# RWKV-7 chunks: a head-pair state without its zero blocks, multiplied in two row halves with one PSUM bank per head

## The chip, the cores and the metric

The kernel runs on one core of one Trainium2 chip. The metric is the device time of one execution in microseconds (us), taken as the median of several runs. TensorE is called PE here, its weight load PEld, VectorE DVE, ScalarE ACT, GpSimd POOL, and SyncE SP.

## What is computed

The reference is a two-layer trunk of width 1024 over 512 tokens. Each layer projects its input with one large matrix, runs two token mixers on the parts (HGRN2 and RWKV-7), gates and merges them, projects again and normalises. The change touches RWKV-7, which has 8 heads of 64 channels, each with a state of 64x64:

```python
def step(S, inp):                       # S_t = S_{t-1}(diag(w) - kk^T (a*kk)) + v^T k ; y = S r
    r_t, w_t, k_t, v_t, kk_t, a_t = inp
    sa = jnp.einsum('bhvk,bhk->bhv', S, -kk_t)
    S = (S * w_t[:, :, None, :] + sa[..., None] * (kk_t * a_t)[:, :, None, :]
         + v_t[..., None] * k_t[:, :, None, :])
    y = jnp.einsum('bhvk,bhk->bhv', S, r_t)
    return S, y
```

The kernel computes this in 8 chunks of 64 tokens per layer: within a chunk everything is matrix products, and the state goes from chunk to chunk.

## The kernel before

**The work and its order.** One Python program writes out all instructions for the two layers. The bulk of TensorE's work is the projections: `proj` (L258) multiplies a weight tile by all 512 tokens in 24 matmuls of 512 columns each (L267, L268, L272), with weights split into a high and a low part by ACT (L122) and POOL (L127, `wl`). These projections serve as filler: `weave` (L283) takes a number of filler matmuls from a list of counts, then lets the main generator issue its next piece. For the chunks the counts are `WCH` (L33): 0, 3, 3, 1, 7, 5, 5 filler matmuls before the pieces of one chunk, 24 in all. Each engine runs its own instructions in the order written, so the filler stands on TensorE's queue between the products of the chunk.

**One chunk** (`rw_chunk`, L571) handles 8 heads as 4 pairs (`p` is the pair, `h` the head in it; head `h` has its 64 channels in row half `64*h`). Its pieces, by line:

- L589: 8 products `pg`, 64 rows each, the two heads of a pair in two PSUM banks; DVE masks them into `Gt` (a tile named G, L592).
- L601: 4 transposes; ACT copies them to `bkt` (L603).
- L608, in chunks 1 to 7: the old state times the queries and keys. The state `mbd` is a tile of 128 rows by 4 pairs by 128 columns; for each pair its two 64x64 blocks stand on the diagonal and the other two blocks are zero (a memset at L1076 in each layer). So one full 128-row matmul of 128 columns serves a pair.
- L613: 8 products of 64x64 added to the same bank `py`; DVE scales one row half of 256 columns at a time into `W` (L618, recorded at the helper L127).
- L623: 8 products with `ar` into `psa`; DVE copies one half into `X`, ACT the other (L625).
- L631, in chunks 0 to 6: 8 products for the state's update, each head's 64x64 result on its diagonal place in the bank `pm`; DVE adds it to `gm` and writes `mbd`, one row half at a time (L638, helper L127; L636 in chunk 0); POOL makes the decayed `gm` from it (L640).
- L643: 8 more products into `py`; ACT copies the result to `X` in two instructions of 64x256 (L647). In every second chunk DVE, POOL and ACT work on from there (L650 to L658), towards the group norm and, after the last chunk, the transposes of `rw_final` (L691).

A 32-bit float product is recorded as two passes, so 8 products are x16 in the trace's rows and the 4 of L608 are x8.

**Tiles and pools.** PSUM has 8 banks in three pools: `pj` 2, `rw` 4, `hg` 2 (L94). `py` is of pool `rw`. The tile `mbd` is also used elsewhere, whole, as a 512-column row of conditioning values (`silc`, L174).

Of the kernel before, what the change touches and what calls it, by code (L numbers as in the profile page):

```python
# [16 lines left out]
ALU = mybir.AluOpType  # L17
# [66 lines left out]
def body(ctx, tc, d):  # L84
    nc = tc.nc
    V, A, G, PE = nc.vector, nc.scalar, nc.gpsimd, nc.tensor
# [10 lines left out]
    def st(tag, shape, dt=F32):  # L97
        cnt[0] += 1
        return sp.tile(shape, dt, tag=tag, name=f"{tag}_{cnt[0]}", bufs=BUFS[tag])

    def ps(tag):
        cnt[0] += 1
        return pp.tile([128, 512], F32, tag=tag, name=f"p{tag}_{cnt[0]}", bufs=PB[tag])
# [13 lines left out]
    def cst(name, shape, dt=F32):  # L117
        return cp.tile(list(shape), dt, name=name)

    def act(out, in_, f, scale=1.0, bias=0.0):  # L120
        if f == AF.Copy:
            A.activation(out, in_, f, scale=scale)  # L122
        else:
            A.activation(out, in_, f, scale=scale, bias=bias)  # L124

    def tt(e, o, a, b, op):
        e.tensor_tensor(o, a, b, op=op)  # L127

    def mul(e, o, a, b):
        tt(e, o, a, b, ALU.mult)  # L130
# [4 lines left out]
    def stt(o, a, s, b, op0, op1):  # L135
        V.scalar_tensor_tensor(o, a, s, b, op0=op0, op1=op1)  # L136

    def bc(ap, n):
        return ap.unsqueeze(len(ap.shape)).broadcast_to(list(ap.shape) + [n])
# [4 lines left out]
    mm = PE.matmul  # L144
# [21 lines left out]
    craw = [ps("rw"), ps("rw")]  # L166
    for h in range(2):
        cmm = mm(craw[h], ones[0:1], crow[:, h * 512:(h + 1) * 512], start=True, stop=True)
    mbd = cst("mbd", (128, 4, 128))
    silc = []  # L170

    def c_rows(craw):

        silc[:] = [mbd.rearrange("p a b -> p (a b)"), st("W", [128, 512])]  # L174
        for h in range(2):
            act(silc[h], craw[h], AF.Tanh, scale=0.5)
            stt(silc[h], silc[h], 1.0, craw[h], ALU.add, ALU.mult)
# [171 lines left out]
    rw = {}  # L349
# [11 lines left out]
    gam = cst("gam", (128, 4, 8))  # L361
    d2 = cst("d2", (128, 4, 4, 2))
# [206 lines left out]
    gm = cst("gm", (128, 4, 64))  # L569

    def rw_chunk(l, c):  # L571


        ytm = rw["ytm"]
        par, c4 = c % 2, c // 2
        yo = [64 * (par ^ g) for g in range(2)]
        yrs, zrs = [slice(y, y + 64) for y in yo], [slice(64 - y, 128 - y) for y in yo]
        halves = [slice(256 * g, 256 * g + 256) for g in range(2)]
        heads = [(p + 2 * g, h) for p in range(2) for h in range(2) for g in range(2)]
        hcol = lambda p, h: slice(p * 128 + h * 64, p * 128 + h * 64 + 64)  # L580
        ch = slice(c * 128, (c + 1) * 128)
        ZR, BK, X = rw["ZR"], rw["BK"], rw["vtm"][c]

        yield
        pg = [ps("rw"), ps("rw")]
        for p in range(4):
            for h in range(2):
                hs = slice(64 * h, 64 * h + 64)
                mm(pg[h][:, p * 128:(p + 1) * 128], BK[p][hs, ch], ZR[p][hs, ch], start=p == 0, stop=p == 3)  # L589
        Gt = st("G", [128, 2, 4, 128])  # L590
        for h in range(2):
            mul(V, Gt[:, h].rearrange("p (g a) b -> p g a b", g=2), pg[h].rearrange("p (g a b) -> p g a b", g=2, b=128),  # L592
                gmask(par))
        bkt = None
        if c < 7:
            sk = st("W", [128, 4, 128])
            mul(G, sk, rw["BKb"].rearrange("p a b c -> p a (b c)")[:, :, ch], bc(gam[:, :, c], 128))
            yield
            pb = ps("rw")
            for p in range(4):  # L600
                PE.transpose(pb[:, p * 128:(p + 1) * 128], sk[:, p], ident)  # L601
            bkt = st("bkt", [128, 512])
            A.copy(bkt, pb)  # L603
        yield
        py = ps("rw")
        if c > 0:
            for p in range(4):
                mm(py[:, p * 128:(p + 1) * 128], ZR[p][:, ch], mbd[:, p], start=p == 0, stop=False)  # L608
        yield
        for n, (p, h) in enumerate(heads):  # L610
            g = p // 2
            z = zrs[g]
            mm(py[z, hcol(p, h)], Gt[yrs[g], h, p, z], X[yrs[g], hcol(p, h)], start=c == 0 and n < 2, stop=n > 5)  # L613
        W = st("W", [128, 512])
        j3 = lambda t: t.rearrange("p (n j) -> p n j", j=64)
        for g in range(2):
            z, o = zrs[g], halves[g]
            mul(V, j3(W[z, o]), j3(py[z, o]), bc(d2[z, c4, 2 * g:2 * g + 2].rearrange("p a b -> p (a b)"), 64))  # L618
        yield
        psa = ps("rw")  # L620
        for n, (p, h) in enumerate(heads):
            z = zrs[p // 2]
            mm(psa[z, hcol(p, h)], ar[z, h, p, c4], W[z, hcol(p, h)], start=n < 2, stop=n > 5)  # L623
        for g in range(2):
            PK[1 - g](X[zrs[g], halves[g]], psa[zrs[g], halves[g]])  # L625
        yield
        if c < 7:
            pm = ps("rw")
            for p in range(4):
                for h in range(2):  # L630
                    mm(pm[64 * h:64 * h + 64, hcol(p, h)], bkt[:, hcol(p, h)], X[:, hcol(p, h)], start=p == 0, stop=p == 3)  # L631
            for h in range(2):
                hs = slice(64 * h, 64 * h + 64)
                new = pm[hs].rearrange("p (a b) -> p a b", b=128)[:, :, hs]
                if c == 0:
                    V.tensor_copy(mbd[hs, :, hs], new)  # L636
                else:
                    tt(V, mbd[hs, :, hs], new, gm[hs], ALU.add)  # L638
                if c < 6:
                    mul(G, gm[hs], mbd[hs, :, hs], bc(gam[hs, :, c + 1], 64))  # L640
        for n, (p, h) in enumerate(heads):
            y = yrs[p // 2]
            mm(py[y, hcol(p, h)], Gt[:, h, p, y], X[:, hcol(p, h)], start=False, stop=n > 5, skip_group_check=True)  # L643
        if par == 0:
            ytm.append(X)
        for g in range(2):
            A.copy(ytm[-1][64 * par:64 * par + 64, halves[g]], py[yrs[g], halves[g]])  # L647
        if par == 1:

            y = ytm[-1]  # L650
            y3 = y.rearrange("p (h j) -> p h j", j=64)
            s1, s2 = st("sm", [128, 8]), rw["s2"][:, c4]
            V.tensor_reduce(s1, y3, axis=AX.X, op=ALU.add)
            V.tensor_scalar_mul(s1, s1, -1.0 / 64)
            tt(G, y3, y3, bc(s1, 64), ALU.add)
            sq = st("bkt", [128, 512])
            act(sq, y, AF.Square)
            V.tensor_reduce(s2, sq.rearrange("p (h j) -> p h j", j=64), axis=AX.X, op=ALU.add)  # L658
# [329 lines left out]
    for l in range(L):  # L988
# [84 lines left out]
                run(fill)  # L1073
            rkv = []
        ada_next()
        G.memset(mbd, 0.0)  # L1076
        inv = rw_invert()
        next(inv)
        weave(hg_norm(l, oT), fill, WHN)
# [291 lines left out]
```

## Time and profile before

| what | value |
|---|---|
| median of 3 runs | 1013.33 us (1008.05 to 1017.07) |
| the profiled execution's own time | 1013.57 us |
| its span from first to last instruction | 1011.8 us |
| mean granted TensorE clock in it | 0.991 of full speed |
| PE busy | 939.3 us (93% of the span) |
| DVE, POOL, ACT busy | 711.7, 632.4, 452.2 us |
| chunks of layer 0, of layer 1 | about 301 to 392 us, about 790 to 881 us |

The rows in the last section but one come from this execution; times in them count from the span's start. A row of a timeline gives start, duration, engine, line, operation, output and inputs; several of a kind are merged with xcount. A matmul's duration is modelled and includes the way through the array, so that successive matmuls overlap in it: what one costs is read from the starts. "idle before" is the time the engine stood still, and the arrow names what ended it.

### The profile page before, as it was taken

To read this page: it belongs to the slowest core of one execution; us is meant where nothing else is said; L and a number is where in the kernel's file an instruction comes from. 1 tells how busy PE (TensorE), PEld (TensorE's weight loads), DVE (VectorE), ACT (ScalarE), POOL (GpSimd) and SP (SyncE) were. 2 spreads that over 40 slices of the span, in tenths; PEclk is the share of its full clock that TensorE was granted. 3 is DMA by queue.
4 is the path that set the end of the run, shared out by engine and by line. 5 is a ranking of instruction groups with operands and counts; after the bars stand their busy time and mean duration, and the time that the engine had idled before them with its cause. 6 is when DMAs were issued, how large, how long until landed. Compare 5 with 4: busy or idle time off the path is not lost.

```text
span 1011.8 us, 17028 instructions
## 1 busy us (share of the span) xinstructions
PE 939.3 (93%) x6132; PEld 751.6 (74%) x6132; DVE 711.7 (70%) x1265; ACT 452.2 (45%) x920; POOL 632.4 (63%) x738
## 2 busy tenths in 40 slices
PE   7877889999999999999989979999999999999997
PEld 3656768887877777776877868778788777787776
DVE  7889997769974443588777895867699344436667
ACT  3356445556334335333445645446632443453421
POOL 5366646556655557768646566666754566686865
PEclk9999999999999999999999999999999999999999
DMA  8824532222321112665632632232233111254322
GB/s 315 306 63 136 177 126 74 88 80 80 97 75 45 52 46 65 186 213 169 186 132 63 205 87 77 70 94 63 64 99 90 53 43 53 85 177 157 115 74 83
DMA packets 61750, 112.85 MB, mean 112 GB/s; under 512 B 6865, under 2 KB 11361, under 8 KB 61666
## 3 DMA queue, kind: packets, MB, share of 16 engines
q1 hardware_dynamic: 57778, 105.12, 34.1%
q10 hardware_dynamic: 3888, 6.64, 2.0%
q8 instruction: 48, 0.79, 0.3%
q14 instruction: 36, 0.29, 0.1%
HBM read 106.49 MB, written 5.25 MB: 110 GB/s over the span
## 4 chain that ended last, share of the span: by engine, by line
PE 47%; DVE 24%; POOL 9%; DMA 7%; issue 7%; ACT 6%; POOLq 0%; SPq 0%; DVEq 0%; ACTq 0%
PE ppj L272 11%; PE ppj L267 10%; PE ppj L268 10%; POOL wl L127 5%; DVE u L127 4%; DVE z L308 2%; DVE B L308 2%; DVE hl L127 2%; DMA raw<-in_w_out 2%; DMA z<-in_w_ada 2%; ACT wh L122 2%; PE prw L589 2%; POOL hl L127 1%; PE prw L608 1%; DVE pu L136 1%
## 5 line engine op out<-in xcount | busy, mean ns | idle before, releaser
L127 POOL TENSOR_TENSOR wl<-raw,wh 128x256 fp32r<-128x256 f32 x460 | 384.5, 859 | 245.1 <-ACT wh L122 158.5
L122 ACT ACTIVATE wh<-raw 128x512 fp32r<-128x512 f32 (+1 forms) x233 | 144.0, 622 | 162.6 <-PE ppj L268 87.2
L267 PE MATMUL ppj<-B,wh 128*128 128x512 f32 x432 | 175.4, 406 | 5.3 <-DVE u L136 2.2
L268 PE MATMUL ppj<-B,wh 128*128 128x512 f32 x432 | 172.3, 399 | 0.0
L267 PE MATMUL ppj<-A,wh 128*128 128x512 f32 x400 | 161.1, 403 | 0.2 <-ACT wh L122 0.2
L268 PE MATMUL ppj<-A,wh 128*128 128x512 f32 x400 | 159.6, 399 | 0.0
L272 PE MATMUL ppj<-B,wl 128*128 128x512 f32 x432 | 125.9, 401 | 0.6 <-DVE dvsh L127 0.4
L272 PE MATMUL ppj<-A,wl 128*128 128x512 f32 x400 | 116.9, 401 | 4.6 <-POOL wl L127 4.6
L267 PEld LDWEIGHTS ppj<-B,wh 128*128 128x128 f32 x432 | 81.9, 190 | 24.0 <-ACT wh L122 3.8
L272 PEld LDWEIGHTS ppj<-B,wl 128*128 128x128 f32 x432 | 80.3, 190 | 19.0 <-POOL wl L127 2.4
L268 PEld LDWEIGHTS ppj<-B,wh 128*128 128x128 f32 x432 | 82.0, 190 | 14.9
L272 PEld LDWEIGHTS ppj<-A,wl 128*128 128x128 f32 x400 | 73.3, 188 | 22.8 <-POOL wl L127 8.1
L267 PEld LDWEIGHTS ppj<-A,wh 128*128 128x128 f32 x400 | 75.5, 189 | 16.0 <-ACT wh L122 0.6
L268 PEld LDWEIGHTS ppj<-A,wh 128*128 128x128 f32 x400 | 75.7, 189 | 13.7
L127 POOL TENSOR_TENSOR hl<-hl,u 128x256 f32<-128x256 f32 x40 | 31.9, 797 | 20.7 <-DVE u L774 7.8
L127 DVE TENSOR_TENSOR W<-prw,d 64x256 f32<-64x256 f32 x32 | 13.5, 422 | 36.9 <-PE prw L613 26.0
L136 DVE SCALAR_TENSOR_TENSOR pr<-ppj,prm,pr 128x511 f32<-128x511 f32 x22 | 16.4, 747 | 31.8 <-ACT pr L124 31.8
L127 DVE TENSOR_TENSOR t<-t,t 128x144 f32<-128x144 f32 (+29 forms) x62 | 35.1, 566 | 2.1
L308 DVE CUSTOM_DVE_ANT_0 z<-z,mbd,prm 128x512 f32<-128x512 f32 x32 | 31.8, 995 | 3.9 <-DMA z<-in_w_ada 3.8
L127 DVE TENSOR_TENSOR hl<-hl,u 128x256 f32<-128x256 f32 x64 | 32.6, 524 | 1.4 <-ACT u L792 1.3
L308 DVE CUSTOM_DVE_ANT_0 z<-z,W 128x512 f32<-128x512 f32 x32 | 29.0, 905 | 2.7 <-DMA z<-in_w_ada 2.7
L127 DVE TENSOR_TENSOR G<-prw,cc 128x512 f32<-128x512 f32 x32 | 20.6, 684 | 12.0 <-PE prw L589 11.8
(480 smaller groups left out, 1967.4 us busy)
## 6 DMA issues: line engine op xcount, KB each, us to landing
raw<-in_w_in SPq DMA_DIRECT2D x182, 256.0 KB, 2.6
z<-in_w_ada SPq DMA_DIRECT2D x64, 256.0 KB, 3.2
B<-in_w_ada SPq DMA_DIRECT2D x16, 512.0 KB, 5.9
raw<-in_w_br SPq DMA_DIRECT2D x32, 256.0 KB, 2.7
raw<-in_w_out SPq DMA_DIRECT2D x32, 256.0 KB, 2.6
u<-in_x SPq DMA_DIRECT2D x8, 256.0 KB, 4.5
o<-in_w_in SPq DMA_DIRECT2D x14, 128.0 KB, 4.2
t<-in_xt SPq DMA_DIRECT2D x6, 256.0 KB, 3.2
```

What stands on the lines that cost most here:

```text
L122: A.activation(out, in_, f, scale=scale)
L127: e.tensor_tensor(o, a, b, op=op)
L136: V.scalar_tensor_tensor(o, a, s, b, op0=op0, op1=op1)
L267: yield mm(o, w, xh, start=half == 0 and k == 0, stop=False)
L268: yield mm(o, w, xl, start=False, stop=False)
L272: yield mm(o, w, xh, start=False, stop=half == n - 1 and k == 3)
L308: V.tensor_tensor_reduce(out=w[h], in0=w[h], in1=silc[h], scale=0.5, scalar=0.0 if h else init, op0=ALU.mult, op1=ALU.add, accum_out=part[ ...
L589: mm(pg[h][:, p * 128:(p + 1) * 128], BK[p][hs, ch], ZR[p][hs, ch], start=p == 0, stop=p == 3)
L608: mm(py[:, p * 128:(p + 1) * 128], ZR[p][:, ch], mbd[:, p], start=p == 0, stop=False)
```

## The change

The state is kept without its zero blocks: `mbd` becomes 128 rows by 4 pairs by 64 columns, each head in its own row half, inside a tile `sil` that also serves the old second use. The state product (L608) becomes 8 matmuls of 64 rows and 64 columns instead of 4 of 128 rows and 128 columns, alternating between the two row halves; head 0 of each pair writes one PSUM bank, head 1 another. These two banks are of pool `hg` instead of one of pool `rw`. Since the results of a half now stand in two banks, DVE's scaling into `W` and ACT's copies to `X` become four instructions of 64x128 each; since the state has no gaps, DVE's update and POOL's decay become one instruction of 128x256 each. The memset goes.

```diff
-    mbd = cst("mbd", (128, 4, 128))
+    sil = cst("sil", (128, 512))
+    mbd = sil[:, 0:256].rearrange("p (a b) -> p a b", b=64)
...
-        py = ps("rw")
+
+        py = [ps("hg"), ps("hg")]
+        pcol = lambda p: slice(p * 64, p * 64 + 64)
         if c > 0:
             for p in range(4):
-                mm(py[:, p * 128:(p + 1) * 128], ZR[p][:, ch], mbd[:, p], start=p == 0, stop=False)
+                for h in range(2):
+                    hs = slice(64 * h, 64 * h + 64)
+                    mm(py[h][:, pcol(p)], ZR[p][hs, ch], mbd[hs, p], start=p == 0, stop=False)
         yield
         for n, (p, h) in enumerate(heads):
             g = p // 2
             z = zrs[g]
-            mm(py[z, hcol(p, h)], Gt[yrs[g], h, p, z], X[yrs[g], hcol(p, h)], start=c == 0 and n < 2, stop=n > 5)
+            mm(py[h][z, pcol(p)], Gt[yrs[g], h, p, z], X[yrs[g], hcol(p, h)], start=c == 0 and n < 4, stop=n > 3)
         W = st("W", [128, 512])
-        j3 = lambda t: t.rearrange("p (n j) -> p n j", j=64)
+        by_head = lambda t, r, g, h: t[r].rearrange("p (a b j) -> p a b j", b=2, j=64)[:, 2 * g:2 * g + 2, h]
+        pair = lambda t, r, g: t[r, 128 * g:128 * g + 128].rearrange("p (a j) -> p a j", j=64)
         for g in range(2):
-            z, o = zrs[g], halves[g]
-            mul(V, j3(W[z, o]), j3(py[z, o]), bc(d2[z, c4, 2 * g:2 * g + 2].rearrange("p a b -> p (a b)"), 64))
+            z = zrs[g]
+            for h in range(2):
+                mul(V, by_head(W, z, g, h), pair(py[h], z, g), bc(d2[z, c4, 2 * g:2 * g + 2, h], 64))
...
-                    mm(pm[64 * h:64 * h + 64, hcol(p, h)], bkt[:, hcol(p, h)], X[:, hcol(p, h)], start=p == 0, stop=p == 3)
-            for h in range(2):
-                hs = slice(64 * h, 64 * h + 64)
-                new = pm[hs].rearrange("p (a b) -> p a b", b=128)[:, :, hs]
-                if c == 0:
-                    V.tensor_copy(mbd[hs, :, hs], new)
-                else:
-                    tt(V, mbd[hs, :, hs], new, gm[hs], ALU.add)
-                if c < 6:
-                    mul(G, gm[hs], mbd[hs, :, hs], bc(gam[hs, :, c + 1], 64))
+                    mm(pm[64 * h:64 * h + 64, pcol(p)], bkt[:, hcol(p, h)], X[:, hcol(p, h)], start=p == 0, stop=p == 3)
+            new = pm[:, 0:256].rearrange("p (a b) -> p a b", b=64)
+            if c == 0:
+                V.tensor_copy(mbd, new)
+            else:
+                tt(V, mbd, new, gm, ALU.add)
+            if c < 6:
+                mul(G, gm, mbd, bc(gam[:, :, c + 1], 64))
...
-            mm(py[y, hcol(p, h)], Gt[:, h, p, y], X[:, hcol(p, h)], start=False, stop=n > 5, skip_group_check=True)
+            mm(py[h][y, pcol(p)], Gt[:, h, p, y], X[:, hcol(p, h)], start=False, stop=n > 3, skip_group_check=True)
...
-            A.copy(ytm[-1][64 * par:64 * par + 64, halves[g]], py[yrs[g], halves[g]])
+            for h in range(2):
+                A.copy(by_head(ytm[-1], slice(64 * par, 64 * par + 64), g, h), pair(py[h], yrs[g], g))
...
-        G.memset(mbd, 0.0)
```

On TensorE's queue in chunk 1 of layer 0, the state product stands between two filler matmuls (`ppj`) before. `B` is the tile with queries and keys, `mbd` the state:

```order
L601 MATMUL prw_3245<-cc,W_3233 128x128 x3
L268 MATMUL ppj_3166<-A_167,wh_3237 128x512
L608 MATMUL prw_3253<-mbd,B_602 128x128 [waits PE_49,Activation_49]
L608 MATMUL prw_3253<-mbd,B_602 128x128 x3
L267 MATMUL ppj_3166<-A_167,wh_3237 128x512
L268 MATMUL ppj_3166<-A_167,wh_3237 128x512
```

The same place in the changed kernel, whose lines are numbered a few higher (`phg_3255` and `phg_3256` are the two banks, `sil` holds the state):

```order
L602 MATMUL prw_3247<-cc,W_3235 128x128 x3
L269 MATMUL ppj_3168<-A_167,wh_3239 128x512
L613 MATMUL phg_3255<-sil,B_602 128x64 [waits DVE_49,PE_49,Activation_49]
L613 MATMUL phg_3256<-sil,B_602 128x64 [waits PE_49,Activation_49]
L613 MATMUL phg_3255<-sil,B_602 128x64
L613 MATMUL phg_3256<-sil,B_602 128x64
L268 MATMUL ppj_3168<-A_167,wh_3239 128x512
L269 MATMUL ppj_3168<-A_167,wh_3239 128x512
```

The last two L613 rows of this piece come three times more in a row; the filler around the product has not moved. On DVE's queue in the same chunk, before:

```order
L127 TENSOR_TENSOR W_3273<-prw_3253,d_152 64x256 [waits PE_49,Pool_49]
L127 TENSOR_TENSOR W_3273<-prw_3253,d_152 64x256
L625 COPY X_899<-prw_3296 64x256 [waits PE_49]
L136 SCALAR_TENSOR_TENSOR z_3277<-u_3278,z_3277 128x512 [waits Activation_49]
L127 TENSOR_TENSOR mbd<-prw_3312,gm 64x4x64 [waits DVE_49,PE_49]
L127 TENSOR_TENSOR mbd<-prw_3312,gm 64x4x64 [waits DVE_49]
L653 TENSOR_REDUCE sm_3335<-X_898 128x8 [waits Activation_49]
```

And after:

```order
L127 TENSOR_TENSOR W_3280<-phg_3255,d_152 64x2x64 [waits PE_49,Pool_49]
L127 TENSOR_TENSOR W_3280<-phg_3256,d_152 64x2x64 [waits PE_49]
L127 TENSOR_TENSOR W_3280<-phg_3255,d_152 64x2x64
L127 TENSOR_TENSOR W_3280<-phg_3256,d_152 64x2x64
L632 COPY X_899<-prw_3305 64x256 [waits PE_49]
L136 SCALAR_TENSOR_TENSOR z_3286<-u_3287,z_3286 128x512 [waits Activation_49]
L127 TENSOR_TENSOR sil<-prw_3321,gm 128x256 [waits DVE_49,PE_49]
L659 TENSOR_REDUCE sm_3344<-X_898 128x8 [waits Activation_49]
```

The scaling into `W` is four instructions where it was two, the state's update one where it was two; nothing else changes its place there. SP's queue is the same word for word.

## Rows read from the trace of the kernel before

**Rows 1.** Page, part 1: busy time of TensorE, share of the span.

```profile
PE 939.3 (93%) x6132; PEld 751.6 (74%) x6132; DVE 711.7 (70%) x1265; ACT 452.2 (45%) x920; POOL 632.4 (63%) x738
```

**Rows 2.** Window of one chunk: length, then busy us of PE, PEld, DVE, ACT, POOL, clock, DMA share.

```profile
336.60:347.70 11.10, 11.10 (x117) 8.55 (x116) 4.08 (x8) 3.57 (x8) 6.38 (x9) 1.00 0.19 49
```

**Rows 3.** Timeline of TensorE, chunk 4 of layer 0.

```profile
347.44 0.40 PE L272 MATMUL ppj<-A,wl 128*128 128x512 f32 x1
347.77 1.16 PE L589 MATMUL prw<-B,B 64*128 64x128 f32 x16
348.86 0.50 PE L267 MATMUL ppj<-A,wh 128*128 128x512 f32 x1
349.19 0.39 PE L268 MATMUL ppj<-A,wh 128*128 128x512 f32 x1
349.42 0.39 PE L267 MATMUL ppj<-A,wh 128*128 128x512 f32 x1
...
350.01 0.48 PE L268 MATMUL ppj<-A,wh 128*128 128x512 f32 x1
350.32 1.05 PE L608 MATMUL prw<-mbd,B 128*128 128x128 f32 x8
351.13 0.47 PE L267 MATMUL ppj<-A,wh 128*128 128x512 f32 x1
351.44 0.39 PE L268 MATMUL ppj<-A,wh 128*128 128x512 f32 x1
```

**Rows 4.** Lines L589 and L613: count, ns min/median/max, first and last start.

```profile
L589 PEld LDWEIGHTS prw<-B,B x128: 182/188/188, 301.1 to 381.8; 64*128 64x128 f32 x128
L589 PE MATMUL prw<-B,B x128: 272/272/373, 301.1 to 381.9; 64*128 64x128 f32 x128
...
L613 PEld LDWEIGHTS prw<-X,G x256: 129/135/135, 307.0 to 874.7; 64*64 64x64 f32 x128
L613 PE MATMUL prw<-X,G x256: 218/218/267, 307.0 to 874.7; 64*64 64x64 f32 x128
```

**Rows 5.** Timeline of PE and DVE around the scaling into W, chunk 3.

```profile
341.51 0.40 PE L272 MATMUL ppj<-A,wl 128*128 128x512 f32 x1
341.84 0.68 PE L613 MATMUL prw<-X,G 64*64 64x64 f32 x16
...
342.62 0.88 DVE L127 TENSOR_TENSOR W<-prw,d 64x256 f32<-64x256 f32 x2 [3.46 <-issue]
342.79 0.39 PE L267 MATMUL ppj<-A,wh 128*128 128x512 f32 x1
...
343.80 0.68 PE L623 MATMUL prw<-W,ar 64*64 64x64 f32 x16
```

**Rows 6.** Groups by line and shape: count, busy us, mean ns, idle before.

```profile
L127 DVE TENSOR_TENSOR G<-prw,cc 128x512 f32<-128x512 f32 x32 | 20.6, 684 | 12.0 <-PE prw L589 11.8
L508 ACT COPY X<-prw 64x128 f32<-64x128 f32 x64 | 16.6, 260 | 14.0 <-PE prw L504 13.3
...
L127 DVE TENSOR_TENSOR W<-prw,d 64x256 f32<-64x256 f32 x32 | 13.5, 422 | 36.9 <-PE prw L613 26.0 <-issue 10.4
...
L127 DVE TENSOR_TENSOR ar<-prw,d 128x256 f32<-128x256 f32 x16 | 6.0, 412 | 0.2 <-PE prw L497 0.2
```

**Rows 7.** Instructions of tile mbd: count, ns min/median/max, first and last start.

```profile
L127 POOL TENSOR_TENSOR gm<-mbd,gam x24: 615/619/623, 313.0 to 860.1; 64x256 f32<-64x256 f32 x24
L127 DVE TENSOR_TENSOR mbd<-prw,gm x24: 416/422/429, 324.3 to 870.5; 64x256 f32<-64x256 f32 x24
```

**Rows 8.** Waits of PE in the chunks, layer 0, then layer 1: us, times, longest.

```profile
PE prw L631 <- ACT X L625: 1.1, 2, 0.6
...
PE prw L631 <- ACT X L625: 1.6, 3, 0.6
```

**Rows 9.** ACT's copies of L647, and TensorE after the last chunk of layer 1.

```profile
L647 ACT COPY X<-prw x32: 364/367/372, 312.9 to 880.7; 64x256 f32<-64x256 f32 x32
...
890.07 0.44 PE L691 MATMUL prw<-cc,X 128*128 128x128 f32 x2 [0.28 <-POOL X L127]
```

More of the change, by code (lines that the diff above doesn't have):

```diff
@@ L168, in body @@
         cmm = mm(craw[h], ones[0:1], crow[:, h * 512:(h + 1) * 512], start=True, stop=True)
-    mbd = cst("mbd", (128, 4, 128))
+    sil = cst("sil", (128, 512))
+    mbd = sil[:, 0:256].rearrange("p (a b) -> p a b", b=64)
     silc = []
     def c_rows(craw):
-        silc[:] = [mbd.rearrange("p a b -> p (a b)"), st("W", [128, 512])]
+        silc[:] = [sil, st("W", [128, 512])]
         for h in range(2):
```

## The prediction

> **What bounds the kernel now.** I read first the busy shares of the engines: TensorE is busy for 93% of the span, the next compute engine, DVE, for 70% [rows 1]. A share is a mean over stages, so the second view is the window of one chunk. There the reader sees 11.10 us of PE in a window of 11.10 us, with DVE at 4.08, ACT at 3.57 and POOL at 6.38 us [rows 2]; the windows of the next three chunks give the same 11.10. The third view is TensorE's timeline: projections and the chunk's products follow one another without a wait [rows 3, 5]. So in this stage the queue of TensorE sets the time, DVE, ACT and POOL have from 43% to 68% of it free, and what the change does to PE's own time counts in full, while relief for DVE, ACT and POOL counts only where PE waits for them. In both layers together, PE's own waits in the chunks for the copy before L631 are five, 1.1 and 1.6 us in all [rows 8].
>
> The price of a product is not its duration in a row but the time by which it pushes the projections apart. The step from one projection to the next is 349.42 - 349.19 = 0.23 us. From the projection before L589 to the second after it are 349.19 - 347.44 = 1.75 us with two projections in them, so L589 costs 1.75 - 0.46 = 1.29 us. For L608 it is 351.44 - 350.01 = 1.43, less 0.46: 0.97 us [rows 3]. For L613 it is 342.79 - 341.51 = 1.28, less 0.46 for the one projection before it and the first one after it (at 342.45, not among the rows): 0.82 us [rows 5].
>
> **The state product on TensorE.** The change takes away L608's 8 passes (4 matmuls) of 128 rows by 128 columns of weights and 128 moving columns, and adds 16 passes of 64 rows by 128 columns of weights with 64 moving columns. This happens in chunks 1 to 7 of two layers, 14 times. The rows show nothing of this shape, but both of its neighbours: L589 has the same weights (64 rows, 128 columns) in the same two row halves and two banks, with 128 moving columns; L613 has 64 moving columns with weights of 64 columns.
>
> What a pass of the new shape waits for is read from the weight load. A load of 128 columns lasts 188 ns, one of 64 columns 135 ns: 53 ns more for 64 columns, so 106 ns for 128. The first matmul after a change of shape, which can't hide its load, says the same: 373 instead of 272 ns in L589, 267 instead of 218 in L613 [rows 4]. The 16 passes of L589 take 1.16 us, less 0.27 for the last and 0.10 for the first load, so 0.79 us over 7 steps, 0.113 us per pair of passes: the two row halves do work side by side, each pair in the time of one load or one stream of 128 columns, which are equally long. L613's step, (0.68 - 0.22 - 0.05)/7, is 0.059 us [rows 4, 5]. The new product halves the stream but not the load. I take the load as its limit: a step of 0.11 us, 8 steps, as L589. Only the last pass is shorter, by 272 - 218 = 54 ns [rows 4]. So 1.29 - 0.05 = 1.24 us instead of 0.97, 0.27 us more; 14 times, **+3.8 us**. Bounds: the whole of L589, +0.32, 14 times +4.5 us; L613's price, 0.82, -0.15, 14 times -2.1 us. I choose near L589 because the load is the thing that the two have in common, and its length was measured twice.
>
> Half of this price is no arithmetic: 8 steps of 0.113 make 0.90 of L589's 1.29 us, the other 0.39 are the way into the smaller shape and back, with a first load in the open each time [rows 3, 4]. L608 in full 128-row shape, like the projections around it, paid only 0.97 - 8 x 0.11 = 0.09. The new form pays what L589, L613 and L623 pay already. Here the Trainium skill has rules for both sides. "TensorEngine Tiling (Array Packing)", section Overview, promises up to twice the speed when the contraction is 64 or less; by it the product's 0.9 us would halve, and 14 times 0.45 us would be an estimate of 6 us gained. "TensorE: Matmul & The Clock Gate", section "LDWEIGHTS (loading the stationary operand)": a load takes its time by the columns of the weights, not their rows, so halving the rows gains nothing there; the trace's 188 ns at 64 rows agrees, against 135 for half the columns [rows 4].
>
> **The other products** keep their shapes and counts: L613, L623, L631, L643 write other columns or banks, with the same tiles. Cost 0. L613's two row halves still alternate.
>
> **Scaling into W.** Two DVE instructions of 64x256 (422 ns each, 0.88 us for two) become four of 64x128. From 684 ns for 512 columns and 412 for 256, a column costs 1.06 ns, so one of 128 columns takes 422 - 136 = 0.29 us [rows 6], four some 1.16 to 1.2 us, 0.3 us later in all. Behind it on PE's queue stand L623, then projections. L623 started at 343.80, when the projection before it was through; the old W ended at 343.50, 0.30 us before [rows 5]. The new one ends at about 343.8, and L623's first matmuls need only its first and third part. I take 0. Bounds: no gain, since W was not what L623 waited for; at most four whole old instructions, 1.69 us from 342.62, so 344.31: 0.5 us in each of 16 chunks, 8 us.
>
> **State update and decay.** Two of 422 ns on DVE become one of about 0.41, two of 619 ns on POOL one [rows 6, 7]: 0.4 and some 0.5 us less per chunk. The cover that made the old ones free is L589 and what follows it up to the next L608, 350.32 - 347.77 = 2.55 us of PE's work [rows 3], behind L643 and three projections. So 0; if that cover were gone, the shorter forms would gain their 0.9 us per chunk (the fourth rival). A gain is bounded by the waits of L631, 2.7 us [rows 8], but these end with ACT's copy after a gate's work, not with the state. The memset was on POOL, which had spare time: 0.
>
> **Copies to X.** Two of 367 ns on ACT become four of about 260, the time of a 64x128 copy from PSUM [rows 6, 9]: 0.3 us more per chunk. ACT has 7 us free in a chunk [rows 2]. Only after the last chunk does PE come near to this chain: in layer 1 it waited 0.28 us for POOL before L691 [rows 9], so there 0.3 us come on top; layer 0 shows no such wait. **+0.3 us.** The new banks of pool `hg` come free with these copies, which follow L643 and so run beside the three projections ahead of L589; the next state product is 2.55 us behind L589's start [rows 3]. 0.
>
> **Sum.** 3.8 + 0.3 = 4.1 us. The profiled execution took 1013.57 us, 0.2 us above the median of the runs shown: 1013.57 + 4.1 = 1017.7, or 1017.4 by the median. I say **1017.6 us**, 0.4% slower. A change within 1%, about 10 us, is about what a measurement of this kernel can't tell from none: its three runs lie 9 us apart.
>
> **Rivals.** First: the load is no limit, because it runs ahead across the row halves, and the stream of 64 columns sets the pace. Then the product costs L613's 0.82, and 1013.57 - 2.1 + 0.3 = 1011.8 us. For it speaks that L613 does reach 0.059 us; against it that its loads have half the columns. Its chance is 0.15. (It is what the Trainium skill's rule of twice the speed, named above, would come to in this kernel.) Second, on the slower side: W takes the place of PE's queue as what L623 waits for. It decides from 0.30 us per instruction of 64x128 on, (343.80 - 342.62)/4; at the full 0.42 it costs 8 us more, 1025.7 us. For it: my 0.29 is just under the point. Against: the first part needs only one bank and can start before L613 has ended. 0.10. Third: the change doesn't do what it says, and the halves run one after the other. 16 steps of 0.113 and 0.39 make 2.2 us instead of 0.97, 14 times 1.23 is 17.2, so 1031 us. L589's pairs speak against it: 0.04. Fourth: the chain through DVE and POOL does bound the chunks, and 0.4 + 0.5 us go in 12 of them or more: 1013.6 - 11 = 1003 us. The full windows [rows 2] speak against it: 0.03.
>
> **How the numbers follow.** The forecast has 0.68. The range takes in the first rival and most of the way to the second, 1009.5 to 1023.5 us. Faster by over 1% only the fourth rival gives: 0.03. Slower by over 1%: the third, and the second where it costs its most, with a little for noise: 0.11. Within 1%: 0.86.
>
> **What would show it.** In the changed profile, the state product's rows should read 16 passes with weight loads near 188 ns; from the projection before it to the second after it should be 1.70 us instead of 1.43. W's four rows near 0.29 us, and L623 still right behind its projection. Chunks of 11.4 us instead of 11.1. A step below 0.08 us per pair in the state product proves the first rival, a wait of PE for DVE at L623 the second, starts of the two halves 0.1 us apart the third, a chunk shorter than 11 us the fourth.

## The result and the profile after

The changed kernel takes 1019.69 us in the median (1015.56 to 1023.69), the kernel before 1013.33 us; the ratio is 1.0065 with a 95% interval of 1.005 to 1.008. That is 6.6 us, 0.65% slower, within 1%; 1017.6 us was forecast. The profiled execution took 1020.16 us, with a span of 1018.4 us at a mean clock of 0.984.

TensorE's busy time grew by 11 us, DVE's and POOL's fell by 11 and 7 us (page, part 1, of the changed kernel; against [rows 1]):

```profile
PE 950.3 (93%) x6244; PEld 757.5 (74%) x6244; DVE 701.1 (69%) x1283; ACT 454.0 (45%) x952; POOL 625.6 (61%) x724
```

The window from one chunk's start to the next (chunk 4 of layer 0; length, then busy us of PE, PEld, DVE, ACT, POOL, clock, DMA share, GB/s) is again filled by PE, and is 11.42 us where [rows 2] had 11.10:

```profile
345.75:357.17 11.42, 11.42 (x129) 8.63 (x125) 5.43 (x13) 4.18 (x11) 6.73 (x8) 1.00 0.16 47
```

TensorE's timeline in that chunk, the counterpart of [rows 3] (line numbers are a few higher: the projections are L268, L269 and L273 now, the state product L613):

```profile
345.75 0.97 PE L273 MATMUL ppj<-A,wl 128*128 128x512 f32 x3
346.65 1.16 PE L590 MATMUL prw<-B,B 64*128 64x128 f32 x16
...
348.54 0.60 PE L602 MATMUL prw<-cc,W 128*128 128x128 f32 x4
348.89 0.47 PE L269 MATMUL ppj<-A,wh 128*128 128x512 f32 x1
349.29 1.11 PE L613 MATMUL phg<-sil,B 64*128 64x64 f32 x16
350.33 0.50 PE L268 MATMUL ppj<-A,wh 128*128 128x512 f32 x1
350.67 0.39 PE L269 MATMUL ppj<-A,wh 128*128 128x512 f32 x1
```

From the projection before the state product to the second after it are 350.67 - 348.89 = 1.78 us, where [rows 3] had 1.43 and the forecast 1.70. The product itself, line L613 (count, ns min/median/max):

```profile
L613 PEld LDWEIGHTS phg<-sil,B x112: 182/188/188, 314.1 to 383.7; 64*128 64x128 f32 x112
L613 PE MATMUL phg<-sil,B x112: 272/272/320, 314.1 to 383.7; 64*128 64x64 f32 x112
```

Sixteen passes in 1.11 us, less 0.27 for the last and 0.05 for the first load, are 0.79 us over 7 steps: 0.113 us a pair, as L589 had with twice the moving columns [rows 3, 4].

Around the scaling into W (timeline of PE and DVE, the counterpart of [rows 5]) the four DVE instructions end at 353.82, and L630 starts at 354.11, when the projection of 353.79 has nearly run out:

```profile
352.14 0.68 PE L618 MATMUL phg<-X,G 64*64 64x64 f32 x16
...
352.82 1.00 DVE L127 TENSOR_TENSOR W<-phg,d 64x128 f32<-64x128 f32 x4 [2.17 <-PE phg L618]
...
353.79 0.40 PE L269 MATMUL ppj<-A,wh 128*128 128x512 f32 x1
...
354.11 0.68 PE L630 MATMUL prw<-W,ar 64*64 64x64 f32 x16
```

The state's decay and update (tile sil) are one instruction each, as long as one of the two before [rows 7]; the copies to X (line L653) are 260 ns each [rows 6, 9]:

```profile
L127 POOL TENSOR_TENSOR gm<-sil,gam x12: 621/623/627, 310.8 to 863.1; 128x256 f32<-128x256 f32 x12
L127 DVE TENSOR_TENSOR sil<-prw,gm x12: 424/425/426, 322.6 to 874.0; 128x256 f32<-128x256 f32 x12
```

```profile
L653 ACT COPY X<-phg x64: 257/260/263, 310.5 to 885.0; 64x128 f32<-64x128 f32 x64
```

PE's waits in the chunks of layer 0, then of layer 1 (us, times, longest). Those before L638 are 0.1 and 0.2 us longer than before L631 [rows 8]:

```profile
PE prw L638 <- ACT X L632: 1.2, 2, 0.7
PE prw L602 <- ACT ar L567: 0.2, 1, 0.2
...
PE prw L638 <- ACT X L632: 1.8, 3, 0.7
PE prw L697 <- POOL X L127: 0.3, 1, 0.3
PE prw L602 <- ACT ar L567: 0.2, 1, 0.2
```

### The profile page after: what moved, and what is told of

Same layout as the page of the kernel before. It is cut to its first block, busy times and chain, and to the rows that moved or that the text cites. A ratio compares the mean times of both kernels' runs of the same rounds, so it can differ in the third digit from the quotient of the medians.

```text
span 1018.4 us, 17291 instructions
## 1 busy us (share of the span) xinstructions
PE 950.3 (93%) x6244; PEld 757.5 (74%) x6244; DVE 701.1 (69%) x1283; ACT 454.0 (45%) x952; POOL 625.6 (61%) x724
## 4 chain that ended last, share of the span: by engine, by line
PE 50%; DVE 20%; POOL 8%; issue 6%; DMA 6%; ACT 4%; POOLq 0%; SPq 0%; DVEq 0%; ACTq 0%
PE ppj L273 12%; PE ppj L268 11%; PE ppj L269 11%; POOL wl L127 4%; DVE u L127 3%; DVE z L309 2%; DVE hl L127 2%; DMA z<-in_w_ada 2%; PE prw L590 2%; PE phg L613 1%; POOL hl L127 1%; ACT wh L122 1%; DMA raw<-in_w_out 1%; DVE pu L136 1%; DMA raw<-in_w_br 1%
## 5 line engine op out<-in xcount | busy, mean ns | idle before, releaser
L268 PE MATMUL ppj<-B,wh 128*128 128x512 f32 x432 | 174.6, 404 | 5.5 <-ACT wh L122 2.6
L269 PE MATMUL ppj<-B,wh 128*128 128x512 f32 x432 | 171.5, 397 | 0.0
L268 PE MATMUL ppj<-A,wh 128*128 128x512 f32 x400 | 164.0, 410 | 0.5 <-ACT wh L122 0.5
L269 PE MATMUL ppj<-A,wh 128*128 128x512 f32 x400 | 162.3, 406 | 0.0
L273 PE MATMUL ppj<-B,wl 128*128 128x512 f32 x432 | 126.0, 401 | 2.3 <-POOL wl L127 2.2
L273 PE MATMUL ppj<-A,wl 128*128 128x512 f32 x400 | 117.0, 402 | 3.8 <-POOL wl L127 3.8
L268 PEld LDWEIGHTS ppj<-B,wh 128*128 128x128 f32 x432 | 81.5, 189 | 24.5 <-ACT wh L122 4.3
L273 PEld LDWEIGHTS ppj<-B,wl 128*128 128x128 f32 x432 | 79.9, 189 | 21.2 <-POOL wl L127 4.9
L269 PEld LDWEIGHTS ppj<-B,wh 128*128 128x128 f32 x432 | 81.6, 189 | 15.0
L273 PEld LDWEIGHTS ppj<-A,wl 128*128 128x128 f32 x400 | 74.3, 190 | 21.1 <-POOL wl L127 5.8
L268 PEld LDWEIGHTS ppj<-A,wh 128*128 128x128 f32 x400 | 76.9, 192 | 17.4 <-ACT wh L122 1.4
L269 PEld LDWEIGHTS ppj<-A,wh 128*128 128x128 f32 x400 | 77.4, 193 | 14.2
L127 DVE TENSOR_TENSOR W<-phg,d 64x128 f32<-64x128 f32 x64 | 15.7, 284 | 42.3 <-PE phg L618 31.1
L309 DVE CUSTOM_DVE_ANT_0 z<-z,sil,prm 128x512 f32<-128x512 f32 x32 | 32.3, 1010 | 2.9 <-DMA z<-in_w_ada 2.7
L127 DVE TENSOR_TENSOR t<-t,t 128x144 f32<-128x144 f32 (+29 forms) x62 | 32.4, 522 | 2.1
```

The source lines that it names most:

```text
L268: yield mm(o, w, xh, start=half == 0 and k == 0, stop=False)
L269: yield mm(o, w, xl, start=False, stop=False)
L273: yield mm(o, w, xh, start=False, stop=half == n - 1 and k == 3)
L309: V.tensor_tensor_reduce(out=w[h], in0=w[h], in1=silc[h], scale=0.5, scalar=0.0 if h else init, op0=ALU.mult, op1=ALU.add, accum_out=part[ ...
```

## The experiments

Ratios are to the kernel before, run on the same chip; its medians there were 1013.6 to 1014.3 us. The period is that of the chunks 3 to 7, from one L589 (L590) to the next.

| kernel | median us | ratio, 95% interval | chunk period us |
|---|---|---|---|
| before | 1013.33 | 1 | 11.09 |
| changed | 1019.69 | 1.0065, 1.005 to 1.008 | 11.42 |
| behind_pg | 1013.81 | 0.9987, 0.9968 to 1.0006 | 11.02 |
| four_tiles | 1013.86 | 0.9982, 0.996 to 1.0005 | 11.01 |
| twice | 1030.62 | 1.0146, 1.0119 to 1.0172 | 12.29 |
| splits_only | 1016.11 | 1.0009, 0.9992 to 1.0026 | 11.09 |
| after_again | 1020.8 | 1.0061, 1.0039 to 1.0083 | 11.42 |
| memset_back | 1021.46 | 1.0065, 1.0045 to 1.0085 | 11.42 |
| before_l618 | 1028.2 | 1.0131, 1.011 to 1.0152 | 11.72 |
| before_again | 1013.29 | one run | 11.09 |
| banks_only | 1013.06 | 0.9992, 0.9974 to 1.0011 | 11.09 |
| after_rw | 1021.25 | 1.0078, 1.0056 to 1.0099 | 11.42 |
| before_longer | 1019.78 | 1.0069, 1.0053 to 1.0084 | 11.53 |
| before_longer_2 | 1020.88 | one run | 11.53 |

### The way into the small tile and back: behind_pg

```diff
                 mm(pg[h][:, p * 128:(p + 1) * 128], BK[p][hs, ch], ZR[p][hs, ch], start=p == 0, stop=p == 3)
+        py = [ps("hg"), ps("hg")]
+        pcol = lambda p: slice(p * 64, p * 64 + 64)
+        if c > 0:
...
+                    mm(py[h][:, pcol(p)], ZR[p][hs, ch], mbd[hs, p], start=p == 0, stop=False)
         Gt = st("G", [128, 2, 4, 128])
...
```

The same lines go at their old place.

> The changed kernel with the state product moved right behind L590, which has the same tile of 64 rows and 128 columns; everything is computed. Load theory (eight steps of 0.113 us set by the weight loads, and 0.35 us for the way into the small tile and back): the way in and out is paid once for both, so the two together cost 1.24 + 0.90 = 2.1 to 2.2 us where they cost 1.24 + 1.24 to 1.29, chunks are 11.05 to 11.1 us instead of 11.42, and the time is 14 x 0.36 = 5 us under the changed kernel: about 1014.7 us, 1.001 of the kernel before. Rival (the 1.24 us are sixteen passes of 0.078 us each, with nothing for the change of shape): 1.24 us stay, 1019.7 us, 1.006. Rival (the loss of 6.4 us lies in the other parts of the change or outside the chunks): 1019.7 us as well, with a chunk that is shorter. The state (ready at 357.32 in chunk 5 of layer 0, where the product would start at 358.97) and the copies out of the two banks (ready at 358.04) should not be waited for.

TensorE's timeline in its chunk 4; L597 is the state product:

```profile
346.49 0.97 PE L273 MATMUL ppj<-A,wl 128*128 128x512 f32 x3
347.39 1.16 PE L590 MATMUL prw<-B,B 64*128 64x128 f32 x16
348.38 1.01 PE L597 MATMUL phg<-sil,B 64*128 64x64 f32 x16
349.32 0.50 PE L268 MATMUL ppj<-A,wh 128*128 128x512 f32 x1
349.65 0.39 PE L269 MATMUL ppj<-A,wh 128*128 128x512 f32 x1
```

No projection stands between the two, and no wait. The last of the three projections before L590 begins at 347.06 (merged into the first row), and 349.65 - 347.06 - 0.46 = 2.13 us for both, 0.84 more than L590's 1.29 alone. So eight more steps cost 0.84 us, and the other 0.4 to 0.5 us of the product were the change of shape. The chunk is 0.40 us shorter than the changed kernel's, 14 times 5.6 us, and the time came out 0.8% lower, 7.9 us by the two ratios, with 5.5 to 10.3 us inside their intervals. The load theory holds; the rival that charges the passes alone falls.

### Shorter weights: four_tiles

```diff
-                for h in range(2):
-                    hs = slice(64 * h, 64 * h + 64)
-                    mm(py[h][:, pcol(p)], ZR[p][hs, ch], mbd[hs, p], start=p == 0, stop=False)
+                for h, e in ((1, 0), (0, 1), (1, 1), (0, 0)):
+                    hs, zc = slice(64 * h, 64 * h + 64), c * 128 + 64 * e
+                    mm(py[h][64 * e:64 * e + 64, pcol(p)], ZR[p][hs, zc:zc + 64], mbd[hs, p], start=p == 0, stop=p == 3)
+            for h in range(2):
+                A.copy(st("sm", [128, 8])[:, 0:4], py[h][:, 0:256:64])
...
-            mm(py[h][z, pcol(p)], Gt[yrs[g], h, p, z], X[yrs[g], hcol(p, h)], start=c == 0 and n < 4, stop=n > 3)
+            mm(py[h][z, pcol(p)], Gt[yrs[g], h, p, z], X[yrs[g], hcol(p, h)], start=c == 0 and n < 4, stop=n > 3, skip_group_check=c > 0)
```

> The changed kernel with the state product cut into 64x64 tiles: 16 matmuls (32 passes) with loads of 64 columns, head by rows and keys or queries by columns; two small ACT reads of the banks order it before L618, and a wait of PE for ACT at L618 comes with them. Load theory: with 64 columns a load is 135 ns instead of 188 and the step 0.059 as in L618. If four tiles run at once, eight steps make 0.47 us, the product costs L618's 0.82 us, and the time is 14 x 0.42 = 5.9 us under the changed kernel: 1013.8 us, 1.0005 of the kernel before. If only two run at once, sixteen steps make 0.94 us, the product costs 1.24 to 1.3 us as now: 1020 us, 1.007. Rival (not the load but the pair of row halves has a step of 0.113 us in its own right): four at once 1.24 us, two at once 2.1 us, 1020 or 1032 us. The reads are covered by seven projections (1.6 us) unless ACT is busy just then; if not covered, PE waits for ACT at L618.

Its state product in TensorE's timeline, and the line's loads and matmuls:

```profile
358.93 0.47 PE L269 MATMUL ppj<-A,wh 128*128 128x512 f32 x1
359.33 0.69 PE L613 MATMUL phg<-sil,B 64*64 64x64 f32 x32
359.96 0.50 PE L268 MATMUL ppj<-A,wh 128*128 128x512 f32 x1
360.29 0.39 PE L269 MATMUL ppj<-A,wh 128*128 128x512 f32 x1
```

```profile
L613 PEld LDWEIGHTS phg<-sil,B x224: 129/135/135, 314.3 to 381.1; 64*64 64x64 f32 x112
```

Twice as many passes take 0.69 us instead of 1.11: four run at once, and a step with loads of 64 columns is (0.69 - 0.22 - 0.05)/7 = 0.060 us for all four. From projection to second projection are 360.29 - 358.93 = 1.36 us instead of 1.78, 0.42 less, as expected; the chunk is 11.01 us. Same arithmetic, same 64 moving columns, half the load: the load set the step. A fixed price per pass falls too, since at the old pace four passes would have a step of 0.226 us. The two reads by ACT were covered; PE waited for them nowhere. "TensorEngine Tiling (Array Packing)" of the Trainium skill, section Overview, promises up to twice the speed for a contraction of 64 or less. In the 64x128 shape of the change the trace shows none of it: eight steps take 8 x 0.113 = 0.90 us, and L608's eight full passes, 1.05 us [rows 3] less 0.27 for the last over 7 steps, took 0.11 us each. In 64x64 tiles the eight steps take 8 x 0.060 = 0.48 us, so there it agrees; with the way in and out the whole product costs 1.36 - 0.46 = 0.90 us, where L608 cost 0.97. L608's loads and matmuls in the kernel before:

```profile
L608 PEld LDWEIGHTS prw<-mbd,B x56: 187/192/192, 316.0 to 383.6; 128*128 128x128 f32 x56
L608 PE MATMUL prw<-mbd,B x56: 270/275/275, 316.2 to 383.7; 128*128 128x128 f32 x56
```

### Less stream, the same loads: twice

```diff
                     mm(py[h][:, pcol(p)], ZR[p][hs, ch], mbd[hs, p], start=p == 0, stop=False)
+            for p in range(4):
+                for h in range(2):
+                    hs = slice(64 * h, 64 * h + 64)
+                    mm(py[h][:, 256:288], ZR[p][hs, ch], mbd[hs, p, 0:32], start=False, stop=False)
```

> The changed kernel with eight more matmuls right behind the state product: the same weights of 64 rows and 128 columns, but 32 moving columns, into columns of the two banks that nothing reads. Load theory: the added passes have the step of their loads, 0.113 us a pair, and pay no way in or out: 8 x 0.113 = 0.90 us per chunk, 14 times 12.7 us over the changed kernel: 1032.4 us, 1.019 of the kernel before. Rival (the stream of the moving columns sets the pace, 64 columns in 0.113 us): 32 columns take 0.03 to 0.06 us, 0.24 to 0.48 us per chunk, 3.4 to 6.7 us: 1023 to 1026.5 us, 1.010 to 1.013. Rival (the price is the passes' alone, 1.24 us for sixteen): 17.4 us, 1037 us, 1.023.

```profile
353.62 1.11 PE L613 MATMUL phg<-sil,B 64*128 64x64 f32 x16
354.56 1.03 PE L617 MATMUL phg<-sil,B 64*128 64x32 f32 x16
355.53 0.50 PE L268 MATMUL ppj<-A,wh 128*128 128x512 f32 x1
```

The rows are again TensorE's timeline. The added eight steps, L617, make the chunk 12.29 - 11.42 = 0.87 us longer, 0.109 us a step: with a quarter of L589's moving columns the step stays that of the load. In time it cost 1.0146 - 1.0065 of 1014 us, 8.2 us, less than the 12.2 that the chunks add; the intervals of the two ratios leave 5 to 11 us. Against the kernel before the two agree: from the first L589 (L590) to the last L643 (here L652) of each layer twice takes 97.2 and 96.7 us against 88.6 and 89.5, 15.8 us more, and its time is 14.8 us longer. So it is rather the changed kernel's time that holds more than its chunks show; the section on the time between the layers comes back to this. Between stream and load the chunk decides for the load.

### The other parts alone: splits_only, banks_only, after_rw

splits_only changes the kernel before, in W and in the copies to X:

```diff
-            mul(V, j3(W[z, o]), j3(py[z, o]), bc(d2[z, c4, 2 * g:2 * g + 2].rearrange("p a b -> p (a b)"), 64))
+            for h in range(2):
+                mul(V, by_head(W, z, g, h), by_head(py, z, g, h), bc(d2[z, c4, 2 * g:2 * g + 2, h], 64))
...
-            A.copy(ytm[-1][64 * par:64 * par + 64, halves[g]], py[yrs[g], halves[g]])
+            for h in range(2):
+                A.copy(by_head(ytm[-1], slice(64 * par, 64 * par + 64), g, h), by_head(py, yrs[g], g, h))
```

> The kernel before with one part of the change alone: W is scaled in four DVE instructions of 64x128 and the results are copied to X in four ACT instructions of 64x128; state, product and banks stay as before. Load theory (the loss is all in the state product): chunks of 11.08 to 11.1 us as before, L623 right behind its projection, the time within 1 us of the kernel before, 1.000 (at the end of each layer at most 0.3 us more). Rival (the splits delay L623 or L631 and carry part of the loss of 6.4 us): chunks of 11.2 us or more, 2 to 6 us slower, 1.002 to 1.006, with waits of PE for DVE at L623 or for ACT at L631.

Its groups by line and shape show the split forms, 284 and 260 ns:

```profile
L127 DVE TENSOR_TENSOR W<-prw,d 64x128 f32<-64x128 f32 x64 | 15.7, 284 | 36.9 <-PE prw L613 32.8 <-PE ppj L272 3.8
L649 ACT COPY X<-prw 64x128 f32<-64x128 f32 x64 | 13.5, 260 | 11.2 <-PE prw L644 11.0
```

Chunks stay at 11.09 us, save one of 11.20 in which W came 0.1 us late for L624. By the ratio the splits cost 0.9 us, with nothing and 2.6 us inside the interval: nothing of the loss in the chunks, and at most 2.6 us of the whole.

banks_only takes the old py from pool hg, after_rw the new two from pool rw:

```diff
-        py = ps("rw")
+        py = ps("hg")
```

```diff
-        py = [ps("hg"), ps("hg")]
+        py = [ps("rw"), ps("rw")]
```

> The kernel before with one part of the change alone: its one bank py comes from pool hg instead of rw. Between the chunk stages of the two layers (from the last L643 of layer 0 to the first L589 of layer 1) the three traces with the old state product took 400.9 to 401.7 us, seven with the new one 401.9 to 406.4. Theory (the banks cost nothing, as forecast; the rest outside the chunks is the timing of weight loads, another one in each execution): chunks of 11.08 us, 401 to 402 us between the stages, ratio 0.999 to 1.001. Rival (the moved banks change the turn in which pools rw and hg hand out banks, and something outside the chunks waits longer): 403.5 to 406 us between the stages, 2 to 4 us more, ratio 1.002 to 1.004.

> The changed kernel with that part undone: the two banks of the state product's results come from pool rw. Theory (the banks cost nothing): chunks of 11.42 us, unless L590 or L602 of the next chunk has to wait for a bank until ACT has copied the results (in the changed kernel 358.04, when L590 starts at 358.07), between the stages 402 to 406 us as in the other kernels with the new product, ratio 1.004 to 1.008. Rival (the turn of the banks costs 3 us outside the chunks): 401 to 402 us there, 3 us under the changed kernel, ratio 1.003. On the other side: where a bank is waited for, PE idles before L590 behind ACT, some 0.1 to 0.5 us per chunk, 1.5 to 8 us more.

Neither period moved, and neither ratio left that of its parent kernel. The banks cost and gain nothing in the chunks, and nothing in the time beyond the 2 us that the intervals leave.

### A smaller change of shape: before_l618

```diff
-WCH = (0, 3, 3, 1, 7, 5, 5)
+WCH = (0, 3, 3, 8, 0, 5, 5)
```

> The changed kernel with the state product moved seven projections later, directly ahead of L618 (eight projections before it, none between the two); L618 itself stays behind the same projections. Theory (0.35 us of the product's 1.24 are the way into the small tile and back, about 0.24 in and 0.11 out): the way out and a part of the way in go, L613 and L618 together cost 1.8 to 1.95 us instead of 2.06, chunks are 11.2 to 11.3 us, 14 x 0.11 to 0.25 = 1.5 to 3.5 us under the changed kernel. Rival (going from one small tile to another costs as much as through a projection, because the first load stands in the open either way): 2.06 us and no gain. A rival on the other side: W starts as before but reads banks that are filled later; it should not, since L618 ends where it did.

```profile
351.43 0.85 PE L273 MATMUL ppj<-A,wl 128*128 128x512 f32 x3
352.21 1.10 PE L613 MATMUL phg<-sil,B 64*128 64x64 f32 x14
353.25 0.45 PE L618 MATMUL phg<-X,G 64*64 64x64 f32 x8
353.62 0.43 PE L613 MATMUL phg<-sil,B 64*128 64x64 f32 x2
353.99 0.45 PE L618 MATMUL phg<-X,G 64*64 64x64 f32 x8
354.36 0.50 PE L273 MATMUL ppj<-A,wl 128*128 128x512 f32 x1
```

A miss, and not the experiment that was meant. As the timeline shows, the recorded order put L618's first half before the last matmul of L613 once no projection stood between them: three changes between small tiles instead of one. A single pair of passes, 0.113 us as a step, took 353.99 - 353.62 = 0.37 us. The chunk grew by 0.30 us. It shows that a change from one small shape to another isn't free either; what a single one costs stays open.

### Chunk 0: memset_back

```diff
+        G.memset(sil, 0.0)
         inv = rw_invert()
```

> The changed kernel with the removed memset put back at its place, once per layer (its result is overwritten before it is read). Theory (without this 0.52 us on POOL's queue the chain of the inversion reaches ar earlier, so that L602 of chunk 0 in layer 1 waits 0.8 instead of 2.0 us): 2.0 us at L602 there again, 1.2 us more, 1 to 2 us over the changed kernel, ratio about 1.005 to 1.008. Rival (the state's shorter instructions, its banks or its new tile gain it): 0.8 us at L602, no change in the time.

PE's waits in the chunks of layer 1 in this kernel:

```profile
PE prw L602 <- ACT ar L567: 1.4, 1, 1.4
```

The wait is back at 1.4 us, where the changed kernel had 0.2. But it is a wait of two values that also changes by itself. In layer 1 the kernels with the memset showed 1.4 us in six traces of seven (0.2 in before_longer_2), those without it 0.2 us or none in six of seven (1.4 in before_l618). In layer 0 it was 0.2 and 0.3 us in the changed kernel's first trace and in banks_only, and 1.4 or 1.5 in the other twelve. So the memset seems to shift the odds of some 1.2 us, but with an exception on either side it isn't settled; the time itself, 1.0065 against 1.0061 and 1.0065, can't tell.

### Between the layers: after_again, before_again, before_longer

before_longer is the kernel before, with half of its state product done twice:

```diff
         if c > 0:
+            for p in range(2):
+                mm(py[:, p * 128:(p + 1) * 128], ZR[p][:, ch], mbd[:, p], start=p == 0, stop=p == 1)
             for p in range(4):
```

> The changed kernel once more, unaltered, for a second trace and a second ratio. Theory (in the chunk stages the change costs 14 x 0.35 us of state product and some 0.8 us of waits behind ACT's copies, and gains 1.2 us in chunk 0 of layer 1; chunk 0 of layer 0 and all that lies outside the chunks differ from one execution to the next): chunks of 11.42 us, the time from the first L590 to the last L648 is 90 to 91 us in both layers together with 0.8 us at L602 in chunk 0 of layer 1, but 2.1 us at L602 in chunk 0 of layer 0, where the first trace had 0.9; the ratio is 1.003 to 1.007. Rival (the change costs 3 to 4 us outside the chunks, by a path not yet seen): from the last L648 of layer 0 to the first L590 of layer 1 again 403 us or more, to the end again 126 us or more, and the ratio 1.006 or more.

> The kernel before once more, for a second trace. Theory: chunks of 11.08 to 11.10 us, 2.0 to 2.1 us at L601 in chunk 0 of both layers, 178 us for both chunk stages; outside the chunks it differs from the first trace by some us, as executions of one kernel do (from the last L643 of layer 0 to the first L589 of layer 1 400.9 us in the first trace, from the last L643 to the end 124.2). Rival (outside the chunks the kernel before always takes these times, so that 403.6 and 126.5 in the changed kernel are the change's): 400.9 and 124.2 us again, within 0.5 us.

> The kernel before with chunks made longer by nothing but TensorE's own work: two of the four matmuls of L608 are done twice (the first results are overwritten). Four traces of kernels with the old state product took 400.9 to 401.9 us from the last L643 of layer 0 to the first L589 of layer 1, eight with the new one 401.9 to 406.4 (404.3 in the mean), with the same instructions in the same order there. In the chunks: 2 x 0.22 = 0.44 us more each, 14 times 6.2 us. Theory (when the chunks end later against the weight loads, the stage behind them meets these at another point and waits differently): 403 to 406 us between the stages, and 8 to 10 us over the kernel before in all, ratio 1.008 to 1.010. Rival (the 3 us belong to something else of the new product): 401 to 402 us between the stages, 6 us, ratio 1.006.

> The same kernel as before_longer for a second trace, since single traces between the stages differ by up to 1 us with the old product and 4.5 us with the new one. Theory: 403 to 406 us between the stages again. Rival: 401 to 402 us again. If the two traces lie on both sides, the question stays open.

From the starts of the first L589 (L590) and the last L643 (L648) of each layer, in us:

| trace | layer 0 | between | layer 1 |
|---|---|---|---|
| before, before_again | 88.6, 88.6 | 400.9, 401.7 | 89.5, 89.5 |
| changed, after_again | 90.0, 91.2 | 403.6, 406.4 | 90.7, 90.7 |
| before_longer, before_longer_2 | 91.8, 91.8 | 400.4, 401.4 | 92.3, 91.1 |

The chunk stages take 3.8 us more in after_again than in before_again, 2.6 more in the first pair, in which chunk 0 of layer 0 had the short wait. By the traces the rest of the loss lies between the layers. All six traces with the old product have 400.4 to 401.9 us there, the eight with the new one 401.9 to 406.4 (after_rw 404.9, memset_back 404.5, before_l618 406.0, behind_pg 404.6, four_tiles 401.9, twice 402.5). The instructions and their order on each engine are the same there; PE waits at other places for weights, which ACT and POOL split when their loads land: in the 110 us behind the chunks ACT waited 11.4 us for loads of `in_w_br` before, and 16.2 us in after_again. Longer chunks don't explain it: before_longer has 400.4 and 401.4. Nor do the splits (401.4), the banks (401.9) or the memset. Since behind_pg, with 404.6 us in its trace, is yet as fast as the kernel before in its timed runs, a trace is no measure of this stretch. The granted clock doesn't explain it either: it was at half, 1.2 GHz, for 17.1 us of the stretch in banks_only, with 401.9 us, and for 13.7 us in after_again, with 406.4.

Another comparison narrows it down: the time lost by the ratio, less what the chunk stages of both layers grew by in the trace. What is left is 4.0 us in the changed kernel and 2.4 in after_again, 1.6 in memset_back, 4.0 in after_rw and 2.2 in before_l618, but 0.5 in behind_pg, -0.2 in four_tiles and -1.0 in twice. These three have the changed kernel's tile, banks, splits and update too. By the intervals of the ratios and the waits in chunk 0 each of these differences can be off by 2 to 3 us, so this is a hint, and no more, that the open part doesn't come from what the kernels share. Its cause stays open. From the last L643 (L648) to TensorE's end the traces have 123.0 to 126.8 us, old and new products mixed (before 124.2, before_again 125.6, changed 126.5, after_again 124.3).

## Why the prediction was right, point by point

- **What bounds the kernel.** Right. The chunks are full of PE work before and after, DVE and POOL lost 11 and 7 us of work without a gain in the period, and every change of PE's own time came through: 0.33 us in the changed kernel, 0.44 in before_longer, 0.87 in twice.
- **The state product.** The mechanism was right and the size a little off: "1.24 us instead of 0.97, 0.27 us more; 14 times, +3.8 us". The step, 0.113 us, and the load, 188 ns, came as forecast. From projection to second projection it was 1.78 us, not 1.70: 1.32 instead of 0.97 by the forecast's own reading, and the chunk grew by 0.33 us, 14 times 4.6 us. The 0.08 us are nearly all in the way in: the first pass starts when the projection ahead has nearly run out (349.29, its row ends at 349.36), and that projection, behind the transposes, lasts 0.47 us; the one ahead of L589 lasts 0.40 [rows 3]. The upper bound given, the whole of L589, was too low for that reason, by 0.01 to 0.03 us. One reading was wrong without touching the sum: the 0.39 us that are no arithmetic are three tenths of L589's 1.29, not half.
- **Scaling into W, update, decay, banks.** Cost 0, as forecast: splits_only and banks_only leave the period at 11.09 us. Update and decay were not run alone, but the product's 0.35 us leave them nothing of the 0.33 us by which the chunk grew. W's parts were 284 ns against an estimate of 0.29 us, and overlap to 1.00 us for four, so W ends 0.29 us ahead of L630 where the forecast left next to nothing. What was not foreseen is 0.3 us more in all in the five waits before L638. splits_only and banks_only don't have it and after_rw does, so neither splits nor banks bring it alone; its cause stays open.
- **Copies to X.** Forecast +0.3 us at the end of layer 1; the wait before L697 is 0.3 us as before L691 [rows 9], so nothing is seen of it in the changed kernel. In the one trace of splits_only the wait was 1.0 us.
- **What the sum left out.** On the gaining side some 1.2 us in chunk 0 of layer 1, which the removed memset may have brought, priced at 0 because POOL had time; on the other side the 2 to 3 us between the layers that stay open. With the 0.3 us before L638 the chunks' sum is 4.6 + 0.3 - 1.2 = 3.7 us, against 3.8 in the second pair of traces and 4.1 forecast; the time by the ratios, 6.2 and 6.6 us, has the open part on top. That the chunks' sum came so near is luck in part: 0.8 us too little for the product, 0.3 us of waits not foreseen and 0.3 us of copies not seen stand against a gain of 1.2 us that was priced at 0. The forecast explains some 4 of the 6.4 us. It also held that a change of this size can't be told from none; the interval of the ratio, 1.005 to 1.008, does tell it.
- **The rivals.** The first (the stream sets the pace) fell by the step of 0.113 us, and by twice and four_tiles. The second (W) fell: L630 starts behind its projection, with no wait for DVE. The third (halves one after the other) fell: pairs of passes run in one step. The fourth (DVE and POOL bound the chunks) fell: their work shrank and the chunks grew.

## What to carry to other kernels

Leaving zeros out pays only if the thing that sets TensorE's step gets shorter: here that was the weight load, which goes by the columns of the weights (192 ns for 128 rows and 188 ns for 64 at 128 columns, 135 ns at 64 columns), so halving the rows and the moving columns bought nothing, and cutting the weights to 64 columns (four_tiles) halved the step and took 0.42 us off the product's 1.32. A product in a small tile shape pays some 0.4 us for the way in and out between full-size matmuls; put it next to one of the same shape (behind_pg) and that is paid once. Either version wins back what the change lost, 0.8% against the changed kernel, and ends level with the kernel before: the intervals, 0.9968 to 1.0006 and 0.996 to 1.0005, include 1.

## What the runs showed that the prediction didn't have

- Four 64x64 tiles load and multiply side by side: four passes with four loads of 135 ns each take one step of 0.060 us, the time of two passes in L613 of the kernel before.
- Behind loads of 128 columns 32 moving columns cost as much as 128: a step of 0.109 us against 0.113.
- A single pair of passes squeezed between two runs of another small shape took 0.37 us, three times its step.
- The same instructions in the same order took 400.4 to 406.4 us between the layers, by the trace; differences of 1 us outside the stage that a change touches can't be read from one pair of traces.
